# Attention logits: the low part of the keys against the high queries alone, on half the rows, two heads side by side

## The chip, the cores and the metric

The kernel runs on one NeuronCore of a Trainium2 chip. The metric is the device time of one execution in microseconds. TensorE (PE in the profile) does the matmuls, and its weight loads have a row of their own (PEld); VectorE (DVE), ScalarE (ACT) and GpSimd (POOL) work on rows of 128 partitions; SyncE (SP) issues most DMAs. Matmul results land in PSUM, which has eight banks of 512 fp32 columns.

## The reference

One layer on 1024 tokens of width 1024, in fp32: an input projection, an mLSTM mixer and a sparse attention mixer beside each other, a gated merge, and a feed-forward block. What matters here are the logits of the attention mixer. It has 8 heads of 64 dimensions in 2 groups that share keys; a block of queries is multiplied with three sets of keys (compressed, selected, windowed):

```python
q = q_in.reshape(B, T, G, R, dh).transpose(0, 2, 3, 1, 4) * (dh ** -0.5)
...
lc = (jnp.einsum('bgrqd,bgcd->bgrqc', qb, kc_).astype(jnp.float32)
      + table[:, :, rel_bucket(t[:, None] - cmp_end[None, :])])
...
ls = jnp.einsum('bgrqd,bgqnd->bgrqn', qb, k_g).astype(jnp.float32) + bias_s
...
lw = jnp.einsum('bgrqd,bgkd->bgrqk', qb, k_wb).astype(jnp.float32) + table[:, :, rel_bucket(dist)]
```

Each set goes through a masked softmax and is multiplied with its values; three gates weigh the sums. With 16 blocks of 64 keys and the 16 best chosen, all causal blocks are selected, so the selected branch is plain causal attention.

## The kernel before

**Precision.** Matmuls run in a rounded fp32 format (F32R), in which one pass is too coarse. So each operand is held as a high part (rounded) and a low part (the remainder), and a product is made of several passes: the dense products of three (lines 277 to 279), the logits of two. For the logits the queries' parts are stacked: in a tile QA of one head, rows 0 to 63 hold the high part of the 64 dimensions and rows 64 to 127 the low part (load_pair, line 1001). The keys are stacked twice: KH has the high part of the keys in both halves, KL the low part in both. A pass over 128 rows with KH gives (high q + low q) x high k, and a pass with KL gives (high q + low q) x low k.

**Units.** The attention stage (lines 1130 to 1499) works through 32 units: four pairs of heads, and in each the eight query blocks of 128 in the order 0, 7, 1, 6, 2, 5, 3, 4. A unit makes logits for two branches ("w": up to five blocks of windowed keys, with 64 compressed columns behind the last; "s": all blocks up to its own) and two heads (r = 0, 1). s_job (line 1145) allocates a score buffer of 1024 columns, which is two PSUM banks; there are two such buffers, used in turn. It issues the matmuls on lines 1164 and 1165, at most 512 columns each, so a block row of up to 640 or 1024 columns takes two pairs of them. Then VectorE adds the bias and finds the row's minimum (line 1191, low), ScalarE takes the exponential (line 1195), the rows are scaled, TensorE transposes them (line 1246), ScalarE and VectorE split the result in high and low (lines 1251 and 1255), and TensorE multiplies both with the values (lines 1266 and 1268).

**Order of the work.** A planner writes the order of each engine out before anything is issued. Every step is an Op with an engine, a cost in ns and dependencies; build_s and build_t (lines 1310 and 1356) make them, and a list scheduler (line 1455) takes the step that can start first, with a priority among those that can. When TensorE has nothing that can start within 120 ns, a piece of a dense product is placed instead: three matmuls of 512 columns of one of ten merge tiles (line 1430, c_dense, lines 277 to 279 with the tile name d). Six more merge tiles are computed after the stage. A score buffer comes free when low has read it: s_free keeps those steps, and the logits of the next head but one depend on them.

**Queues.** The QA and key tiles of the next pair are loaded through GpSimd's queue, and the bias tiles through SyncE's, when the last low of a pair is placed.

Of the kernel before, what the change touches and what calls it, by code (L numbers as in the profile page):

```python
# [8 lines left out]
F32 = mybir.dt.float32  # L9
# [5 lines left out]
P = 128  # L15
T = 1024
# [16 lines left out]
KB = 192  # L33
# [124 lines left out]
def body(ctx, tc, a, out, stop=None, dbg=None):  # L158
    nc = tc.nc
# [41 lines left out]
    d_q = [tc.dram_tile([P, 2, T], F32, name=f"d_q{j}") for j in range(4)]  # L201
# [104 lines left out]
    for nm, j in order_b1:  # L306
        c = {"kc": (C_KC, C_VC), "ks": (C_KS, C_KW)}[nm][j] if nm in ("kc", "ks") else colof[nm] + P * j
# [28 lines left out]
    with ExitStack() as sa:  # L336
# [12 lines left out]
        rows = ap_.tile([N_ROW, P], F32, name="rows")  # L349
# [638 lines left out]
    KS, QA, FB, FW = {}, {}, {}, {}  # L988
# [6 lines left out]
    def load_pair(p):  # L995
        g = p // 2
        for r in range(2):
            h = 2 * p + r
            q = kq.tile([P, T], F32R, name=f"QA{h}", tag=f"QA{r}", bufs=2)
            for z in range(2):  # L1000
                nc.gpsimd.dma_start(q[64 * z:64 * z + 64, :], d_q[p][64 * r:64 * r + 64, z, :])
            QA[h] = q
        if p % 2 == 0:
            for j in (1, 0):
                m = KB if j == 1 else P
                kh = kq.tile([P, NT, m], F32R, name=f"KH{g}{j}", tag=f"KH{j}", bufs=1)
                kl = kq.tile([P, NT, m], F32R, name=f"KL{g}{j}", tag=f"KL{j}", bufs=1)
                gs = slice(64 * g, 64 * g + 64)
                for t_, d_ in ((kh, d_kh), (kl, d_kl)):
                    for z in range(2):  # L1010
                        nc.gpsimd.dma_start(t_[64 * z:64 * z + 64, :, 0:P], d_[j][gs, :].rearrange("p (b c) -> p b c", c=P))
                KS[g, j] = (kh, kl)
            if g > 0:
                behind(g)
        for r in range(2):
            h = 2 * p + r
            f = kq.tile([P, T], F32, name=f"FB{h}", tag=f"FB{r}", bufs=1)
            w = kq.tile([P, 640], F32, name=f"FW{h}", tag=f"FW{r}", bufs=1)
            for t_, o_, n_ in ((f, 127, T), (w, FX + 127, 640)):
                d_ = d_rep[h][0:1, :]  # L1020
                nc.sync.dma_start(t_, bass.AP(tensor=d_.tensor, offset=d_.offset + o_, ap=[[RW - 1, P], [1, n_]]))
            FB[h], FW[h] = f, w
# [107 lines left out]
    with ExitStack() as sc:  # L1130
        cp = sc.enter_context(tc.tile_pool(name="stC", bufs=1, reuse_waits="tile"))
        psC = sc.enter_context(tc.tile_pool(name="psC", bufs=1, space=PSUM, reuse_waits="tile"))
# [6 lines left out]
        units = [(p, i) for p in range(4) for i in order]  # L1139
        NU = len(units)  # L1140
        nwin = lambda i: min(i + 1, 5)
        ncmp = lambda i: 8 * i + 7
        SUM, NXT, RS, EX = {}, {}, {}, {}

        def s_job(u, kind, r):

            p, i = units[u]
            g = p // 2
            cs = slice(P * i, P * i + P)
            if kind == "w" and r == 0:  # L1150
                NXT[u] = cp.tile([P, 2, 3], F32, name=f"nx{u}", tag="nx", bufs=3)
                SUM[u] = cp.tile([P, 2, 3], F32, name=f"sm{u}", tag="sm", bufs=3)
                RS[u] = cp.tile([P, 2, 3], F32, name=f"rs{u}", tag="rs", bufs=3)
            nx, sm = NXT[u], SUM[u]
            s = psC.tile([P, T], F32, name=f"S{u}{kind}{r}", tag="S", bufs=2)
            b = 1 if kind == "s" else 2
            kh, kl = KS[g, b - 1]
            q_ = QA[2 * p + r]
            e = cp.tile([P, T if b == 1 else 640], F32, name=f"E{u}{kind}{r}", tag="E" + kind, bufs=4)
            EX[u, kind, r] = e  # L1160
            f = FB[2 * p + r]

            def logits(o, k_, last):
                nc.tensor.matmul(o, q_[:, cs], k_(kh), start=True, stop=False)
                nc.tensor.matmul(o, q_[:, cs], k_(kl), start=False, stop=True)

            if b == 1:
                n, o0 = P * (i + 1), 0
                for c0 in range(0, i + 1, 4):
                    m = min(4, i + 1 - c0)  # L1170
                    logits(s[:, P * c0:P * (c0 + m)], lambda k: k[:, c0:c0 + m, :], False)
                rows_ = []
            else:

                nw = nwin(i)
                n, o0 = P * nw, P if nw == 4 else 0
                if nw > 1:
                    logits(s[:, o0:o0 + n - P], lambda k: k[:, i + 1 - nw:i, 0:P], False)
                logits(s[:, o0 + n - P:o0 + n - P + KB], lambda k: k[:, i, :], True)
                if r == 0:  # L1180
                    EX[u, "c"] = cp.tile([P, 2, P], F32, name=f"E{u}c", tag="Ec", bufs=3)
                ec, nn = EX[u, "c"], ncmp(i)
                nc.gpsimd.memset(ec[:, r, nn:P], 0.0)
                y0 = 31 + 16 * (56 - 8 * i)
                rows_ = [(ec[:, r, 0:nn], s[:, o0 + n:o0 + n + nn], f[:, y0:y0 + 16 * (nn - 1) + 1:16], r, 0)]
            bias = f[:, 896 - P * i:896 - P * i + n] if b == 1 or i < 4 else FW[2 * p + r]
            rows_.insert(0, (e[:, 0:n], s[:, o0:o0 + n], bias, r, b))

            def low():
                for e_, s_, f_, q, b in rows_:  # L1190
                    nc.vector.tensor_tensor_reduce(e_, s_, f_, 1.0, 1.0e29, ALU.add, ALU.min, nx[:, q, b:b + 1])

            def exp():
                for e_, s_, f_, q, b in rows_:
                    nc.scalar.activation(e_, e_, AF.Exp, bias=nx[:, q, b:b + 1], scale=-1.0, accum_out=sm[:, q, b:b + 1])

            return low, exp
# [96 lines left out]
        chain = {"S": [], "T": [], "V": []}  # L1294
# [3 lines left out]
        def push(op):  # L1298
            queues[op.eng].append(op)
            if op.alt:  # L1300
                queues[op.alt[0]].append(op)
            return op
# [4 lines left out]
        s_free = []  # L1307
        pair_at = {}

        def build_s(u):  # L1310
            p, i = units[u]
            ops = {}
            for k, r in (("w", 0), ("w", 1), ("s", 0), ("s", 1)):
                b = {"w": 2, "s": 1}[k]
                box = {}

                def emit(u=u, k=k, r=r, box=box):
                    box["low"], box["exp"] = s_job(u, k, r)


                if b == 1:
                    n, parts = P * (i + 1), [min(512, P * (i + 1) - c) for c in range(0, P * (i + 1), 512)]
                else:
                    n, parts = P * nwin(i), [P * (nwin(i) - 1)] * (nwin(i) > 1) + [KB]
                cost = 2 * sum(max(109.0, m / 2.4 + 13.0) for m in parts)
                deps = []
                if len(s_free) >= 2:
                    deps.append(s_free[-2])
                if u >= 2:
                    deps.append(("T", u - 2, b))  # L1330
                if u % 8 == 0 and k == "w" and r == 0:
                    deps.append(("pair", p))
                deps += chain["S"]
                so = push(Op("PE", cost, deps, emit, (u, 1)))
                chain["S"] = [so]
                nr, n = (2, n + ncmp(i)) if b == 2 else (1, n)
                tt = push(Op("DVE", nr * 180.0 + 1.044 * n, [so], lambda box=box: box["low"](), (u, 1)))
                s_free.append(tt)
                ex = push(Op("ACT", nr * 290.0 + 0.833 * n, [tt], lambda box=box: box["exp"](), (u, 1)))
                ops[k, r] = ex  # L1340
                if r == 1:
                    part = 0 if k == "w" else 1
                    de = [ops[k, 0], ex]
                    todo = scale(u, part)
                    rs = push(Op("DVE", 400.0, de, todo[0][0], (u, 2)))
                    bl = [2, 2, 0, 0] if part == 0 else [1, 1]
                    scd = {}
                    for bb, (fn, _) in zip(bl, todo[1:]):
                        nn = (ncmp(i), P * (i + 1), P * nwin(i))[bb]
                        scd.setdefault(bb, []).append(push(Op("DVE", 70.0 + 0.522 * nn, [rs], fn, (u, 2),  # L1350
                                                               alt=("ACT", 230.0 + 0.833 * nn))))
                    for bb, v in scd.items():
                        ops["sc", bb] = v
            return ops
# [100 lines left out]
        while any(queues.values()):  # L1455
            best = None
            for e in queues:
                cand = None
                for op in queues[e][:LOOK[e]]:
                    r = ready(op, e)  # L1460
# [645 lines left out]
    n = 0  # L2106
# [110 lines left out]
```

## Time and profile before

| what | value |
|---|---|
| time, median of 3 runs (lowest to highest) | 1573.76 us (1572.89 to 1574.58) |
| profiled execution, from its first to its last instruction | 1570.8 us |
| TensorE busy, matmuls | 7922 |
| attention stage, first logits to the last part of the tenth merge tile | 362.8 to 678 us |
| high-key passes (line 1164) and low-key passes (line 1165) | 216 each |
| transposes (line 1246) and value products (lines 1266, 1268) in that stage | 592, and 296 each |

A profile is one execution, and its span leaves out what lies before the first instruction and after the last; the runs' times hold that too. In the views, a matmul is shown from its start to a modelled end, which lies beyond the start of the next one, so the time that one takes from TensorE is read from start to start. PEld rows are the loads of the stationary operand, one for each matmul. A shape such as 128*63 beside a matmul gives the rows and columns of the stationary operand. In the order-in-time view the columns are the start in us, the length in us, the engine, the line, the operation, the tiles (written <- read), the shape and the count, and in brackets the idle time before it with what ended it. In the view by stretch, the columns are the stretch, its length, the busy time of each engine with the number of its instructions, the granted clock, and what the DMA engines moved.

### The profile page before, as it was taken

Reading aid. Unit: us, or ns where it says so; the run is one execution under the profiler, and the core shown is the slowest. Engines: PE = TensorE matmul, PEld = TensorE weight load, DVE = VectorE, ACT = ScalarE, POOL = GpSimd, SP = SyncE. Lnnn points to the kernel's source line nnn. Section 1 sums busy time; section 2 is a strip of 40 time slices with the busy share of each in tenths; the row PEclk is TensorE's granted clock in tenths of the full one; section 3 lists DMA queues with packets and bytes.
Section 4 is the critical chain, followed back from the end, with each engine's and each line's share of the span. In section 5 each row is a group of like instructions: output and inputs, shape, how many; then the busy total and the mean of one; then the engine's idle time right before and its main releaser. Section 6 shows DMA issues by size and latency. Waiting matters only on the chain.

```text
span 1570.8 us, 22156 instructions
## 1 busy us (share of the span) xinstructions
PE 1556.6 (99%) x7922; PEld 1318.7 (84%) x7922; DVE 1053.6 (67%) x2244; ACT 755.2 (48%) x1589; POOL 210.7 (13%) x345
## 2 busy tenths in 40 slices
PE   9999999999999999999999999999999999999997
PEld 7888888888998898888888888888888888888886
DVE  7446662237988787831566677666666666988996
ACT  5115555326888788842445363333333333454443
POOL 4013433430113010123001000000000000000130
PEclk9999999999999999999999999999999999999999
DMA  8107622592328232163556223222222223750302
GB/s 238 44 1 195 168 81 74 171 289 85 83 73 131 79 102 64 48 220 115 162 165 215 96 94 121 94 81 82 92 82 81 81 83 118 268 196 19 108 1 107
DMA packets 145868, 180.91 MB, mean 115 GB/s; under 512 B 9118, under 2 KB 103612, under 8 KB 145758
## 3 DMA queue, kind: packets, MB, share of 16 engines
q1 hardware_dynamic: 135900, 157.01, 32.5%
q0 software_dynamic: 9568, 22.16, 5.6%
q8 instruction: 62, 1.02, 0.3%
q14 instruction: 48, 0.39, 0.1%
q10 hardware_dynamic: 290, 0.33, 0.1%
HBM read 137.43 MB, written 49.90 MB: 119 GB/s over the span
## 4 chain that ended last, share of the span: by engine, by line
PE 95%; DVE 2%; DMA 1%; ACT 1%; issue 0%; POOL 0%; SPq 0%; DVEq 0%; ACTq 0%
PE PS L278 14%; PE PS L277 14%; PE PS L279 14%; PE d L277 9%; PE d L279 8%; PE d L278 8%; PE T L1246 4%; PE obank L1266 2%; PE obank L1268 2%; PE br L279 2%; PE br L277 2%; PE br L278 2%; PE PSA L277 1%; PE PSA L278 1%; PE PSA L279 1%; DVE acc L1649 1%
## 5 line engine op out<-in xcount | busy, mean ns | idle before, releaser
L277 PE MATMUL d<-UTH,whi 128*128 128x512 f32 x544 | 220.5, 405 | 1.0 <-ACT mg L1125 0.7
L279 PE MATMUL d<-UTH,wlo 128*128 128x512 f32 x544 | 212.9, 391 | 0.0
L278 PE MATMUL d<-UTL,whi 128*128 128x512 f32 x544 | 212.3, 390 | 0.0
L1649 DVE TENSOR_TENSOR sl<-PS,sl 128x512 f32<-128x512 f32 x182 | 123.6, 689 | 100.5 <-PE PS L279 100.1
L254 POOL TENSOR_TENSOR wlo<-raw,whi 128x256 fp32r<-128x256 f32 x120 | 93.1, 806 | 309.1 <-ACT whi L248 278.7
L1255 DVE TENSOR_TENSOR TL<-T,TH 128x512 fp32r<-128x512 f32 (+1 forms) x184 | 103.3, 582 | 31.8 <-ACT TH L1251 30.7
L279 PEld LDWEIGHTS d<-UTH,wlo 128*128 128x128 f32 x544 | 102.1, 188 | 22.5
L277 PEld LDWEIGHTS d<-UTH,whi 128*128 128x128 f32 x544 | 102.4, 188 | 17.8 <-ACT mg L1125 2.3
L278 PEld LDWEIGHTS d<-UTL,whi 128*128 128x128 f32 x544 | 102.6, 189 | 15.6
L1251 ACT ACTIVATE TH<-T 128x512 fp32r<-128x512 f32 (+1 forms) x184 | 90.2, 511 | 28.4 <-PE T L1246 25.7
L1649 DVE TENSOR_TENSOR sl<-sl,sl 128x512 f32<-128x512 f32 (+1 forms) x130 | 88.5, 688 | 22.0 <-DMA d_h<-sl 8.8
L1649 POOL TENSOR_TENSOR acc<-acc 128x512 f32<-128x512 f32 x6 | 9.2, 1550 | 618.5 <-DVE acc L1649 618.4
L1652 ACT ACTIVATE sl<-sl 128x512 f32<-128x512 f32 (+1 forms) x77 | 48.7, 633 | 57.5 <-PE PS L278 32.8
L1266 PE MATMUL obank<-TH,VHL 128*128 128x256 f32 x264 | 75.4, 309 | 0.0
L1268 PE MATMUL obank<-TL,VHL 128*128 128x256 f32 x264 | 68.2, 282 | 0.0
L277 PE MATMUL PS<-q 128*128 128x512 f32 x172 | 66.9, 389 | 0.0
L278 PE MATMUL PS<-q 128*128 128x512 f32 x172 | 66.9, 389 | 0.0
L279 PE MATMUL PS<-q 128*128 128x512 f32 x172 | 66.9, 389 | 0.0
L1652 ACT ACTIVATE q<-sl 128x512 fp32r<-128x512 f32 x74 | 43.1, 624 | 42.3 <-PE PS L278 32.1
L1607 DVE TENSOR_TENSOR q<-br,q 128x512 f32<-128x512 f32 x32 | 21.9, 688 | 55.6 <-ACT q L1595 36.7
L1652 ACT ACTIVATE wh<-sl 128x512 fp32r<-128x512 f32 x39 | 24.7, 633 | 58.4 <-PE PS L278 39.5
L1268 PEld LDWEIGHTS obank<-TL,VHL 128*128 128x128 f32 x264 | 50.2, 190 | 1.2 <-DVE TL L1255 0.3
(1314 smaller groups left out, 4330.9 us busy)
## 6 DMA issues: line engine op xcount, KB each, us to landing
raw<-in_w_in SPq DMA_DIRECT2D x33, 512.0 KB, 5.3
d_gu<-sl SPq DMA_DIRECT2D x44, 256.0 KB, 2.2
q<-d_mg SPq DMA_DIRECT2D x32, 256.0 KB, 3.2
d_rep<-d_row POOLq DMA_DIRECT2D x8, 960.0 KB, 11.7
sl<-in_w_down SPq DMA_DIRECT2D x15, 512.0 KB, 3.6
sl<-d_gu SPq DMA_DIRECT2D x15, 512.0 KB, 4.4
ra<-in_w_gate SPq DMA_DIRECT2D x14, 512.0 KB, 3.5
ra<-in_w_up SPq DMA_DIRECT2D x13, 512.0 KB, 3.6
```

Of the source, the lines that this page charges most:

```text
L254: nc.gpsimd.tensor_tensor(lo[:, zs], v[:, zs], cast32(hi)[:, zs], ALU.subtract)
L277: nc.tensor.matmul(ps, ah, bh, start=first, stop=False)
L278: nc.tensor.matmul(ps, ah, bl, start=False, stop=False)
L279: nc.tensor.matmul(ps, al, bh, start=False, stop=last)
L1246: nc.tensor.transpose(pt[:, z, P * r:P * r + P], e, ident)
L1251: nc.scalar.activation(hl[0][:, 0:m], pt[:, 0:m], AF.Copy)
L1255: nc.vector.tensor_tensor(hl[1][:, 0:m], pt[:, 0:m], cast32(hl[0])[:, 0:m], ALU.subtract)
L1266: nc.tensor.matmul(po, vv, th[:, z, :], start=(st[1] == 0), stop=False)
L1268: nc.tensor.matmul(po, vv, tl[:, z, :], start=False, stop=(st[1] == st[2]))
L1607: nc.vector.tensor_tensor(sg[b], ps, sg[b], ALU.mult)
L1649: return pl.step(alts, lambda e: ENG[e].tensor_tensor(out_(), x(), y(), alu), reads, writes, **kw)
L1652: return pl.step((("ACT", cost),), lambda e: nc.scalar.activation(out_(), x(), fn), reads, writes, **kw)
```

## The change

The pass of the low keys takes the high queries alone, over 64 rows instead of 128. The term low q x low k is no longer computed. For head r = 1 of a pair the halves of QA are exchanged when it is loaded: its high part now lies in rows 64 to 127, that of head 0 in rows 0 to 63 as before. So the low-key passes of the two heads use different halves of the array's rows, and they write different score buffers.

The logits of a unit and branch are issued in two steps of the planner. s_first opens the buffer of head 0 and makes its full pass with KH over 128 rows. s_rest opens the buffer of head 1, issues for each segment of columns the 64-row passes of head 0 and head 1 one after the other, and then the full pass of head 1. The planner gives the first step one pass's cost and the second two passes' plus 150 ns. s_first waits for the low of head 0 of the branch before, s_rest for that of head 1. Both low steps depend on s_rest. The windowed logits now lie in the score buffer so that the last block with the compressed keys always begins at column 512.

```diff
             for z in range(2):
-                nc.gpsimd.dma_start(q[64 * z:64 * z + 64, :], d_q[p][64 * r:64 * r + 64, z, :])
+                nc.gpsimd.dma_start(q[64 * (z ^ r):64 * (z ^ r) + 64, :], d_q[p][64 * r:64 * r + 64, z, :])
...
+        def segments(i, kind):
+            if kind == "s":
+                return 0, [(P * c0, min(4, i + 1 - c0), c0) for c0 in range(0, i + 1, 4)]
+            nw = nwin(i)
+            return 4 * P - P * (nw - 1), [(4 * P - P * (nw - 1), nw - 1, i + 1 - nw)] * (nw > 1) + [(4 * P, 0, i)]
+        def s_open(u, kind, r):
             p, i = units[u]
-            g = p // 2
-            cs = slice(P * i, P * i + P)
             if kind == "w" and r == 0:
                 NXT[u] = cp.tile([P, 2, 3], F32, name=f"nx{u}", tag="nx", bufs=3)
                 SUM[u] = cp.tile([P, 2, 3], F32, name=f"sm{u}", tag="sm", bufs=3)
                 RS[u] = cp.tile([P, 2, 3], F32, name=f"rs{u}", tag="rs", bufs=3)
+                EX[u, "c"] = cp.tile([P, 2, P], F32, name=f"E{u}c", tag="Ec", bufs=3)
+            EX[u, kind, r] = cp.tile([P, T if kind == "s" else 640], F32, name=f"E{u}{kind}{r}", tag="E" + kind, bufs=4)
+            SS[u, kind, r] = psC.tile([P, T], F32, name=f"S{u}{kind}{r}", tag="S", bufs=2)
+        def s_part(u, kind, r, rows, seg, start, stop):
+            p, i = units[u]
+            k_ = KS[p // 2, 1 if kind == "w" else 0][rows is not None]
+            rs = slice(0, P) if rows is None else slice(64 * rows, 64 * rows + 64)
+            o, m, b0 = seg
+            src, n = (k_[rs, b0:b0 + m, 0:P], P * m) if m else (k_[rs, b0, :], KB)
+            nc.tensor.matmul(SS[u, kind, r][:, o:o + n], QA[2 * p + r][rs, P * i:P * i + P], src, start=start, stop=stop)
+        def s_first(u, kind):
+            s_open(u, kind, 0)
+            for seg in segments(units[u][1], kind)[1]:
+                s_part(u, kind, 0, None, seg, True, False)
+        def s_rest(u, kind):
+            s_open(u, kind, 1)
+            segs = segments(units[u][1], kind)[1]
+            for seg in segs:
+                s_part(u, kind, 0, 0, seg, False, True)
+                s_part(u, kind, 1, 1, seg, True, False)
+            for seg in segs:
+                s_part(u, kind, 1, None, seg, False, True)
+        def s_job(u, kind, r):
+            p, i = units[u]
             nx, sm = NXT[u], SUM[u]
...
-            kh, kl = KS[g, b - 1]
-            q_ = QA[2 * p + r]
-            def logits(o, k_, last):
-                nc.tensor.matmul(o, q_[:, cs], k_(kh), start=True, stop=False)
-                nc.tensor.matmul(o, q_[:, cs], k_(kl), start=False, stop=True)
...
-                if nw > 1:
-                    logits(s[:, o0:o0 + n - P], lambda k: k[:, i + 1 - nw:i, 0:P], False)
-                logits(s[:, o0 + n - P:o0 + n - P + KB], lambda k: k[:, i, :], True)
...
-                cost = 2 * sum(max(109.0, m / 2.4 + 13.0) for m in parts)
-                deps = []
-                if len(s_free) >= 2:
-                    deps.append(s_free[-2])
-                if u >= 2:
-                    deps.append(("T", u - 2, b))
-                if u % 8 == 0 and k == "w" and r == 0:
-                    deps.append(("pair", p))
-                deps += chain["S"]
-                so = push(Op("PE", cost, deps, emit, (u, 1)))
-                chain["S"] = [so]
+                one = sum(max(109.0, m / 2.4 + 13.0) for m in parts)
+                if r == 0:
+                    deps = [s_free[-2]] if len(s_free) >= 2 else []
+                    if u >= 2:
+                        deps.append(("T", u - 2, b))
+                    if u % 8 == 0 and k == "w":
+                        deps.append(("pair", p))
+                    first = push(Op("PE", one, deps + chain["S"], lambda u=u, k=k: s_first(u, k), (u, 1)))
+                    rest = push(Op("PE", 2 * one + 150.0, [first] + s_free[-1:], lambda u=u, k=k: s_rest(u, k), (u, 1)))
+                    chain["S"] = [rest]
+                def emit(u=u, k=k, r=r, box=box):
+                    box["low"], box["exp"] = s_job(u, k, r)
+                    box["low"]()
                 nr, n = (2, n + ncmp(i)) if b == 2 else (1, n)
-                tt = push(Op("DVE", nr * 180.0 + 1.044 * n, [so], lambda box=box: box["low"](), (u, 1)))
+                tt = push(Op("DVE", nr * 180.0 + 1.044 * n, [rest], emit, (u, 1)))
                 s_free.append(tt)
                 ex = push(Op("ACT", nr * 290.0 + 0.833 * n, [tt], lambda box=box: box["exp"](), (u, 1)))
                 ops[k, r] = ex
```

More of the change, by code (lines that the diff above doesn't have):

```diff
@@ L1142, in body @@
         ncmp = lambda i: 8 * i + 7
-        SUM, NXT, RS, EX = {}, {}, {}, {}
-        def s_job(u, kind, r):
+        SUM, NXT, RS, EX, SS = {}, {}, {}, {}, {}
+        def segments(i, kind):
[4 more added lines that the diff above has]
+        def s_open(u, kind, r):
             p, i = units[u]
-            g = p // 2
-            cs = slice(P * i, P * i + P)
             if kind == "w" and r == 0:
@@ L1154, in s_job @@
+        def s_job(u, kind, r):
+            p, i = units[u]
             nx, sm = NXT[u], SUM[u]
-            s = psC.tile([P, T], F32, name=f"S{u}{kind}{r}", tag="S", bufs=2)
+            s, e, f = SS[u, kind, r], EX[u, kind, r], FB[2 * p + r]
             b = 1 if kind == "s" else 2
-            kh, kl = KS[g, b - 1]
-            q_ = QA[2 * p + r]
-            e = cp.tile([P, T if b == 1 else 640], F32, name=f"E{u}{kind}{r}", tag="E" + kind, bufs=4)
-            EX[u, kind, r] = e
-            f = FB[2 * p + r]
@@ L1163, in logits @@
-            def logits(o, k_, last):
-                nc.tensor.matmul(o, q_[:, cs], k_(kh), start=True, stop=False)
-                nc.tensor.matmul(o, q_[:, cs], k_(kl), start=False, stop=True)
-            if b == 1:
[L1168 to L1172, printed above, removed]
-            else:
-                nw = nwin(i)
-                n, o0 = P * nw, P if nw == 4 else 0
-                if nw > 1:
-                    logits(s[:, o0:o0 + n - P], lambda k: k[:, i + 1 - nw:i, 0:P], False)
-                logits(s[:, o0 + n - P:o0 + n - P + KB], lambda k: k[:, i, :], True)
-                if r == 0:
-                    EX[u, "c"] = cp.tile([P, 2, P], F32, name=f"E{u}c", tag="Ec", bufs=3)
+            o0 = segments(i, kind)[0]
@@ L1182, in s_job @@
+            rows_ = []
+            if b == 1:
+                n = P * (i + 1)
+            else:
+                n = P * nwin(i)
                 ec, nn = EX[u, "c"], ncmp(i)
@@ L1315, in build_s @@
                 box = {}
-                def emit(u=u, k=k, r=r, box=box):
-                    box["low"], box["exp"] = s_job(u, k, r)
                 if b == 1:
```

## The prediction

> **What bounds the kernel now.** I read the page first (span, busy time, chain), then the busy time by stretch inside the attention stage, then the waits of TensorE there, and last the order in time of single matmuls, because the price of this change hangs on the spacing between neighbours.
>
> ```profile
> span 1570.8 us, 22156 instructions
> PE 1556.6 (99%) x7922; PEld 1318.7 (84%) x7922; DVE 1053.6 (67%) x2244; ACT 755.2 (48%) x1589; POOL 210.7 (13%) x345
> PE 95%; DVE 2%; DMA 1%; ACT 1%; issue 0%; POOL 0%; SPq 0%; DVEq 0%; ACTq 0%
> 400.00:440.00 40.00, 40.00 (x276) 36.45 (x274) 34.04 (x115) 33.92 (x92) 5.93 (x16) 1.00 0.41 109
> sum 315.20, PE 314.20 PEld 281.82 DVE 256.39 ACT 252.82 POOL 48.53; mean PE 39.28 PEld 35.23 DVE 32.05 ACT 31.60 POOL 6.07
> PE d L277 <- ACT mg L1125: 0.7, 2, 0.4
> PEld d L277 <- ACT mg L1125: 2.3, 6, 0.5
> ```
>
> The first three lines are the page: 95% of the chain that ended last is TensorE. The next two are the stretches of the attention stage, from 362.8 us (the first logits) to 678 us: TensorE is busy for 314.2 of 315.2 us, VectorE for 256.4, ScalarE for 252.8, and the granted clock is 1.00. The last two are the longest waits of matmuls and of weight loads in this stage: 0.7 and 2.3 us in all. A busy matmul can hide a short gap, since a 512-column one is shown 0.39 us long while the next starts 0.23 us later, but nothing here is a long wait. So time that TensorE gains or loses in the stage goes to the end almost one for one, as long as VectorE (81% busy) keeps up. A gain of 17 us would bring VectorE to 256 of 298 us, so even that could pass through.
>
> The profiled span is 1570.8 us; the median of the three runs is 1573.76, which is 3.0 us more. I add 3.0 to every span.
>
> **What is removed.** The passes of the low keys on line 1165.
>
> ```profile
> 362.80:678.00 315.20, 65.17 (x216) 40.79 (x216) 1.00 0.34 81
> 368.72 0.39 PE L1165 MATMUL S1s<-KL,QA 128*128 128x512 f32 x1
> 368.95 0.39 PE L1164 MATMUL S1s<-KH,QA 128*128 128x512 f32 x1
> 644.64 0.34 PE L1165 MATMUL S30w<-KL,QA 128*128 128x384 f32 x1
> 644.82 0.25 PE L1164 MATMUL S30w<-KH,QA 128*128 128x192 f32 x1
> 644.91 0.28 PE L1165 MATMUL S30w<-KL,QA 128*128 128x192 f32 x1
> 645.02 0.27 PE L1246 MATMUL T<-cst,E28s 128*128 128x128 f32 x1
> 375.94 0.28 PE L1165 MATMUL S2s<-KL,QA 128*128 128x256 f32 x1
> 376.06 0.40 PE L277 MATMUL d<-UTH,whi 128*128 128x512 f32 x1
> 364.09 0.28 PE L1165 MATMUL S0s<-KL,QA 128*128 128x128 f32 x1
> 364.20 0.45 PE L277 MATMUL d<-UTH,whi 128*128 128x512 f32 x1
> ```
>
> The first line is the stretch view of line 1165 alone: 216 matmuls. Their busy time (65 us) overlaps their neighbours, so I count from one start to the next: 0.23 us for 512 columns, 0.18 for 384, 0.11 for 192, 0.12 for 256, 0.11 for 128. From the loops (query blocks 0 to 7, the windowed branch with up to five blocks and 64 compressed columns, the selected branch with block number plus one), a head of one pair has 10 matmuls of 512 columns, 3 of 384, 3 of 256, 8 of 192 and 3 of 128: 27, and 8 heads make the 216. Their time is 8 x (10 x 0.23 + 3 x 0.18 + 3 x 0.12 + 8 x 0.11 + 3 x 0.11) = 35.3 us. All of it is TensorE's own time.
>
> **What is added: the two heads side by side.** The same 216 matmuls come back with 64 rows each, in 108 couples. If both halves of a couple stream together, a couple costs what one pass did: 17.6 us back on. So 17.6 us is the most that this change can gain. If they do not run together it is 35.3 us back on and nothing gained; the trace of before has no matmul of 64 rows, so these are the ends, and I take the first: the operands lie in separate partitions and the results in separate score buffers, so I see nothing that the two share.
>
> **What is added: changing the shape of the array.** Each of the 64 calls of s_rest (32 units, two branches) goes from 128-row matmuls to 64-row ones and back. The trace has such detours, with other small shapes.
>
> ```profile
> 354.36 0.39 PE L278 MATMUL d<-UTL,whi 128*128 128x512 f32 x1
> 354.58 0.39 PE L279 MATMUL d<-UTH,wlo 128*128 128x512 f32 x1
> 354.90 0.44 PE L1103 MATMUL po<-w,hs 128*63 128x64 f32 x4
> 355.27 0.50 PE L277 MATMUL d<-UTH,whi 128*128 128x512 f32 x1
> 355.61 0.39 PE L278 MATMUL d<-UTL,whi 128*128 128x512 f32 x1
> ...
> 354.36 0.19 PEld L279 LDWEIGHTS d<-UTH,wlo 128*128 128x128 f32 x1
> 354.90 0.30 PEld L1103 LDWEIGHTS po<-w,hs 128*63 128x63 f32 x4 [0.35 <-issue]
> 355.27 0.19 PEld L277 LDWEIGHTS d<-UTH,whi 128*128 128x128 f32 x1
> 355.38 0.19 PEld L278 LDWEIGHTS d<-UTL,whi 128*128 128x128 f32 x1
> ...
> 119.84 0.39 PE L279 MATMUL d<-UTH,wlo 128*128 128x512 f32 x1
> 120.16 0.25 PE L812 MATMUL pq<-cst,gall 32*128 32x32 f32 x1
> 120.24 0.22 PE L813 MATMUL pq<-cst,gall 32*128 32x32 f32 x1
> 120.39 0.50 PE L277 MATMUL d<-UTH,whi 128*128 128x512 f32 x1
> 120.73 0.40 PE L278 MATMUL d<-UTL,whi 128*128 128x512 f32 x1
> ...
> 6.40 0.29 PEld L568 LDWEIGHTS G<-MV,ones 1*128 1x128 f32 x2
> 6.51 0.18 PEld L568 LDWEIGHTS G<-MV,ones 1*128 1x128 f32 x1
> ```
>
> Read the weight loads. Between equal shapes a load starts as soon as the matmul before begins (354.36, with the matmul of 354.36), so it is hidden. At a change of shape it starts only after that matmul is through: 354.90 against a slot that fell due at 354.58 + 0.23 = 354.81, so 0.09 us of nothing and then a load in the open; the same on the way back (load at 355.27, the next load 0.11 us later, the next matmul 0.34 after instead of 0.23). "Issue" as the reason says that no other engine was waited for. A whole detour: from 119.84 to 120.73 is 0.89 us, less two ordinary slots of 0.23 is 0.43, and the two 32-column matmuls in it are at most 0.08. From 354.58 to 355.61 is 1.03, less 0.46 is 0.57, and its four matmuls take some 0.22 (0.44 from the first start to the last end, less the 0.22 for which so short a matmul is shown, as on L813). Both leave about 0.35, the second with shorter loads; by parts it is 2 x (0.09 + 0.11) = 0.40. I take 0.38: 64 x 0.38 = 24.3 us.
>
> The Trainium skill, page "TensorEngine Tiling (Array Packing)", section Tiling Modes, says that changing the tiling mode, not merely the tile, drains the engine. The detours above agree with it, with about 0.09 us of nothing on each side; the page gives no figure, and it names no load left in the open, which in these rows costs as much again.
>
> **The second weight load of a couple.** Each half needs its own load. The nearest row is the last of the fence: two loads of L568 are 0.11 us apart. They go to the same rows of the array, so this is the upper end: 64 x 0.11 = 7.0 us (a couple that follows another inside a call loads under the streaming one). The lower end is nothing. I take a third, 2.4 us, since in my case the halves are separate.
>
> The Trainium skill, page "TensorE: Matmul & The Clock Gate", section "Part 3: Packing small matmuls", says that loads overlap with running matmuls when the row groups differ and that such matmuls start about 4 ns apart. By that rule the second load would cost nothing and the sum below would be 6.6 us instead of 9.0 (1580.4 us). No row here shows it.
>
> **What moves.** First and rest together still make one full pass per head. The rest waits until the reduction of the other head of the branch before has read its score buffer; behind it, in order, stand transposes, value products and merge tiles, and VectorE's line 1191 waits for it with both heads. Before, head 0 could be reduced while head 1's logits ran. The cost is between nothing and, if VectorE idles for one couple and its switch in each call (17.6 / 64 + 0.38 = 0.66 us), 42 us; I take nothing, because VectorE has 315.2 - 256.4 = 58.8 us of idle time and TensorE gets later, not earlier. If this cover went, TensorE would stand at the next rest. The changed partition of the QA loads issues the same 16 transfers; nothing for GpSimd's queue, and the planner's own arithmetic costs no time on the chip.
>
> Sum: -35.3 + 17.6 + 24.3 + 2.4 = +9.0 us, between +6.6 and +13.6 with the second load at its ends. Span 1579.8, time 1582.8 us.
>
> **The rivals.** *The switch is cheap.* The diff books 150 ns per call for it. Then 64 x 0.15 = 9.6 us against 17.6 gained: 8.0 us faster, 1565.8 us. Against it: no detour in the trace cost under 0.35 us. For it: none of them has 64 rows by 128 columns. It decides below 17.6 / 64 = 0.28 us per call. The Trainium skill's tiling page, section Overview, gives up to twice the speed for two row tiles; with the switch and the loads at nothing that is the full 17.6, or 1556.2 us. I give this side 0.17.
>
> *The halves do not run together.* Then nothing is gained and the calls pay the switches: -35.3 + 35.3 + 24.3 = +24.3, 1598.1 us. For it: no matmul in this trace is seen beside another. Against: separate rows and separate buffers. 0.12.
>
> *The tie of both heads stalls VectorE*, on top of the forecast: if a fifth of the 42 us shows, 8 us more, some 1591 us. For it: in the stretch quoted VectorE is at 34.0 of 40 us. 0.07.
>
> *It cancels.* A call costs about 0.28 us all told: 1573.8. 0.09.
>
> **How the numbers follow.** The forecast, 1582.8, has 0.55, and 1580 to 1588 is its own range. Together with the two slower rivals that is 0.74 for slower, 0.09 for the same, 0.17 for faster; 0.2% is 3.1 us, about what a measurement can tell. The range goes from 1566, the cheap switch, to 1597, just short of no overlap; what lies outside, the page's full gain and most of the second rival, is under 0.2.
>
> **What would show it.** Right: in the changed trace the first 64-row weight load of a call starts about 0.09 us after the slot at which a matmul was due, marked "issue"; the 128-row load behind the couples does the same; the two halves of a 512-column couple start less than 0.15 us apart and the next matmul follows in under 0.45; busy time of TensorE in the stage stays near all of it and the stage grows by some 9 us, nothing else moves. Wrong: loads hidden across the change of shape (cheap switch), halves 0.23 us apart (no overlap), or long idle rows of VectorE that end with the 64-row matmuls (the tie).

## The result, and the profile after

The changed kernel takes 1591.59 us (median of 4 runs, 1590.56 to 1593.14) against 1573.33 for the kernel before on the same chip: ratio 1.0114, 95% interval 1.01 to 1.0129, or 18.3 us slower. The forecast was 1582.8: the right side and inside the range, but half the size.

The first lines of the page after:

```profile
span 1590.5 us, 22155 instructions
PE 1568.1 (99%) x7922; PEld 1304.6 (82%) x7922; DVE 1064.0 (67%) x2248; ACT 751.2 (47%) x1585; POOL 212.2 (13%) x345
```

The stretch view of the attention stage in two parts, columns as before:

```profile
364.00:664.00 300.00, 296.95 (x1885) 244.37 (x1884) 237.49 (x767) 223.62 (x599) 49.60 (x124) 1.00 0.33 83
664.00:700.00 36.00, 30.31 (x209) 24.71 (x208) 29.43 (x83) 27.57 (x72) 0.29 (x2) 1.00 0.10 23
```

The longest waits of matmuls (PE) and of weight loads (PEld) in this stage, with the total, the count and the longest in us:

```profile
PE T L1262 <- DVE TL L1271: 3.2, 5, 1.2
PE d L277 <- ACT mg L1125: 1.3, 3, 0.6
PE S31s L1170 <- DVE nx L1207: 1.2, 1, 1.2
PE S4s L1170 <- DVE rs L1223: 1.0, 1, 1.0
PEld T L1262 <- DVE TL L1271: 5.5, 8, 1.4
PEld d L277 <- ACT mg L1125: 1.8, 3, 0.7
PEld S31s L1170 <- issue: 1.6, 2, 1.4
PEld S4s L1170 <- PE T L1262: 1.2, 1, 1.2
```

TensorE, which hardly waited before, now waits for VectorE's split (line 1255 before, 1271 now), and in the last 36 us of the stage it is idle for 5.7. Where the stage's time went is seen from the last merge tile inside it and the last output of the attention. These are the evictions of the merge tiles (line 1125) and the output copies (line 1274 before, 1290 after), of before and then of after; the numbers behind the count are the shortest, the median and the longest in ns, and the first and last start:

```profile
L1125 ACT ACTIVATE mg<-d,COLS x20: 687/689/692, 368.6 to 680.2; 128x512 f32<-128x512 f32 x20
L1274 ACT ACTIVATE os<-obank x32: 363/386/388, 373.1 to 677.4; 128x256 f32<-128x256 f32 x32
```

```profile
L1125 ACT ACTIVATE mg<-d,COLS x20: 687/688/692, 370.6 to 667.3; 128x512 f32<-128x512 f32 x20
L1290 ACT ACTIVATE os<-obank x32: 365/384/387, 374.2 to 698.9; 128x256 f32<-128x256 f32 x32
```

Before, fill and attention ended together, at 680 and 677 us. Now the fill is through at 667 and the attention only at 699; for 31 us nothing fills TensorE's holes. (Some 1.7 us of these shifts came in before the stage; see the last section.)

And one call of s_rest, the selected logits of unit 1 with two segments of 512 columns per head, matmuls and then weight loads in order of time (the first two low-key passes, then all four, from two windows of the same view):

```profile
371.94 0.40 PE L279 MATMUL d<-UTH,wlo 128*128 128x512 f32 x1
372.27 0.50 PE L1170 MATMUL S1s<-KL,QA 64*128 64x512 f32 x2
372.27 0.73 PE L1170 MATMUL S1s<-KL,QA 64*128 64x512 f32 x4
372.94 0.73 PE L1170 MATMUL S1s<-KH,QA 128*128 128x512 f32 x2
373.50 0.28 PE L1282 MATMUL obank<-TH,VHC 128*128 128x256 f32 x1
...
372.27 0.19 PEld L1170 LDWEIGHTS S1s<-KL,QA 64*128 64x128 f32 x2 [0.37 <-issue]
372.94 0.30 PEld L1170 LDWEIGHTS S1s<-KH,QA 128*128 128x128 f32 x2 [0.37 <-issue]
```

Two 64-row matmuls stand together in 0.50 us, the length of a single one with its load in the open, and two loads in 0.19, the length of one: the heads do run side by side, and so do their loads. The first load comes 0.10 us after the slot that fell due at 371.94 + 0.23, marked "issue"; the load of the full pass at 372.94 stands in the open too. From 372.17 to the working start of the full pass, 373.50 - 2 x 0.23 = 373.04, the call took 0.87 us for what four passes of 0.23 did in 0.92. This is the best case. Measured the same way from slot to slot, all 64 calls took 41.4 us in place of 35.3: some 6 us of the loss. In the rest of the stage, the time from each matmul's start to the next exceeds the median of its width before by 13.9 us in all; in the kernel before that sum is 3.0. So some 11 of the other 12 us are lost between matmuls elsewhere in the stage.

### The profile page after: what moved, and what is told of

It reads as the page before. It is cut to its first block, busy times and chain, and to the rows that moved or that the text cites. A ratio compares the mean times of both kernels' runs of the same rounds, so it can differ in the third digit from the quotient of the medians.

```text
span 1590.5 us, 22155 instructions
## 1 busy us (share of the span) xinstructions
PE 1568.1 (99%) x7922; PEld 1304.6 (82%) x7922; DVE 1064.0 (67%) x2248; ACT 751.2 (47%) x1585; POOL 212.2 (13%) x345
## 4 chain that ended last, share of the span: by engine, by line
PE 94%; DVE 3%; ACT 1%; DMA 1%; issue 1%; SPq 0%; DVEq 0%; ACTq 0%
PE PS L278 14%; PE PS L277 14%; PE PS L279 14%; PE d L277 8%; PE d L279 8%; PE d L278 8%; PE T L1262 4%; PE obank L1282 2%; PE obank L1284 2%; PE br L277 2%; PE br L278 2%; PE br L279 2%; PE PSA L277 1%; PE PSA L279 1%; PE PSA L278 1%; DVE acc L1664 1%
```

## The experiments

Unless another kernel is named, each difference is taken against the kernel before as measured beside that run (1573.96 us for the full rows, the same half and the two with one more tile; 1572.27 for the lows tied, the true cost, the cut with full rows and 64 rows alone; 1573.14 for the lows not tied and the two changed kernels with the cut; 1572.32 for the fill later).

**Full rows: the order alone.** The changed kernel, its low-key passes over 128 rows again.

```diff
-            rs = slice(0, P) if rows is None else slice(64 * rows, 64 * rows + 64)
+            rs = slice(0, P)
```

> The changed kernel with its low-key passes over all 128 rows again (all four products, as before the change), in the changed order: no 64-row matmul is left, so neither halves side by side nor changes of shape, but the two steps, the tie of both heads and the planner's costs stay. Theory (in the trace the 64 calls cost 6.2 us more than the passes they replace, and the other 12 us come from the order: the fill of merge tiles ends at 667 us and the attention runs on alone until 698): 1583 to 1588 us. Rival (the changes of shape are dearer than the spacings show, and the order is free): 1573 to 1576 us.

Measured: 1588.61 us, ratio 1.0097 (1.0081 to 1.0113), 14.6 us slower with no 64-row matmul at all. Its profile has the same tail as the changed kernel, first by the stretch, then by the last evictions and output copies:

```profile
664.00:700.00 36.00, 30.27 (x194) 25.77 (x193) 26.76 (x76) 24.77 (x64) 2.97 (x6) 0.95 0.13 29
```

```profile
L1125 ACT ACTIVATE mg<-d,COLS x20: 687/690/691, 369.9 to 663.0; 128x512 f32<-128x512 f32 x20
L1290 ACT ACTIVATE os<-obank x32: 362/383/387, 373.5 to 695.9; 128x256 f32<-128x256 f32 x32
```

The granted clock of 0.95 in the first line is 1.00 in the changed kernel: up to 36 x 0.05 = 1.8 us of this run's loss can be clock and not order. With that said, the order of the work, not the arithmetic, is the larger part of the loss.

**Same half: the halves cannot overlap.** Both heads' high queries in rows 0 to 63.

```diff
-                nc.gpsimd.dma_start(q[64 * (z ^ r):64 * (z ^ r) + 64, :], ...
+                nc.gpsimd.dma_start(q[64 * z:64 * z + 64, :], ...
-            rs = slice(0, P) if rows is None else slice(64 * rows, 64 * rows + 64)
+            rs = slice(0, P) if rows is None else slice(0, 64)
```

> The changed kernel with both heads' high queries in rows 0 to 63, so that the two 64-row passes of a couple use the same half and cannot stand beside each other; all else as changed. Theory (halves do stream together, worth half of the removed 35.3 us): 12 to 18 us slower than the changed kernel, 1603 to 1610 us. Rival (they gain nothing by lying in separate halves): 1590 to 1593 us.

Measured: 1606.99 us, ratio 1.0217 (1.0199 to 1.0235). The same call of unit 1 in its profile:

```profile
372.35 0.39 PE L279 MATMUL d<-UTH,wlo 128*128 128x512 f32 x1
372.67 1.19 PE L1170 MATMUL S1s<-KL,QA 64*128 64x512 f32 x4
373.79 0.50 PE L1170 MATMUL S1s<-KH,QA 128*128 128x512 f32 x1
```

Four 64-row passes span 1.19 us instead of 0.73. Against the changed kernel this is 15.4 us (14.8 if each is taken against the kernel before measured beside it): what the side-by-side is worth, near the 17.6 that it could be at most. Against the full rows it is 18.4 us, for 64 changes of shape there and back.

**One more merge tile inside the stage**, in the changed kernel and in the one before.

```diff
-NMC = 10
+NMC = 11
```

> The changed kernel with 11 instead of 10 merge tiles inside the attention stage (5 instead of 6 behind it). Theory (the attention's last 30 us wait for VectorE and ScalarE with nothing to fill them, about 9 us of idle TensorE): 1582 to 1586 us. Rival (the attention is longer everywhere, and a further merge tile only lengthens it): 1590 to 1593 us.

> The kernel before with 11 merge tiles inside the attention stage. Theory (its fill lasts to the end of the attention, only 3 us idle in all): 1572 to 1575 us, no change. Rival (one more tile of fill helps whatever the order): 1565 to 1569 us.

Measured: the changed kernel 1587.06 us, 1.0088 (1.0072 to 1.0104), so 4.5 us better than with ten; the kernel before 1575.63, 1.0014 (1.0004 to 1.0023), 1.7 us worse and a little above what I expected. So the changed order has idle time that fill can use and the one before has none, but one tile gets back less than I had expected.

**Lows tied, and not tied.** The code of the full rows, rearranged so that the first step makes all of head 0's passes and the second all of head 1's, with true costs. In the first run both reductions are planned behind the second step, in the other each behind its own.

```diff
             s_open(u, kind, 0)
             for seg in segments(units[u][1], kind)[1]:
                 s_part(u, kind, 0, None, seg, True, False)
+                s_part(u, kind, 0, 0, seg, False, True)
...
+                s_part(u, kind, 1, None, seg, True, False)
+                s_part(u, kind, 1, 1, seg, False, True)
...
-                tt = push(Op("DVE", nr * 180.0 + 1.044 * n, [rest], emit, (u, 1)))
+                tt = push(Op("DVE", nr * 180.0 + 1.044 * n, [rest if r else first], emit, (u, 1)))
```

The last pair of lines is the difference between the two runs; the first has the line with [rest].

> The order of the kernel before (each head makes its own passes with the high and the low keys over 128 rows, head 1 behind head 0, no 64-row matmul) with one part of the tie: the reductions of both heads are planned behind the second step. The planner's costs are the true ones. Theory (the order's 14.7 us come mainly from head 0 being reduced late): 1582 to 1588 us. Rival (they come mainly from head 0's low-key pass waiting for head 1's buffer): 1573 to 1577 us.

> The run with the lows tied, with that one dependency undone: head 0's reduction is planned behind the first step, head 1's behind the second. Everything else of the changed code stays that is neither the tie nor the 64-row passes (exchanged halves of the queries, the place of the columns in the score buffer, the logits and their reduction emitted in separate steps). Theory (these cost nothing, the tie does): 1572 to 1575 us. Rival (part of the order's cost is theirs): 1577 to 1586 us.

Measured: tied 1585.16 us, 1.0083 (1.006 to 1.0106), 12.9 slower; not tied 1573.09, 1.0002 (0.9993 to 1.0012). One dependency in the planner, with the same matmuls and the same bytes, costs 12 to 13 us. All the rest of the changed code (the exchanged halves, the place of the columns, the separate steps) costs nothing that can be measured.

The 12 us are not all of the kind that the changed kernel loses. This is the stretch from 520 to 540 us, where unit 16 begins and the second group's keys are loaded, of the tied, the untied and the changed kernel, and then two waits of the tied one there:

```profile
520.00:540.00 20.00, 16.91 (x77) 13.33 (x76) 5.88 (x32) 6.79 (x23) 5.46 (x15) 0.91 1.01 169
520.00:540.00 20.00, 19.64 (x121) 16.95 (x120) 16.31 (x71) 16.61 (x51) 3.70 (x11) 1.00 0.22 61
520.00:540.00 20.00, 19.83 (x121) 17.08 (x121) 9.20 (x27) 10.62 (x27) 4.18 (x9) 1.00 0.75 199
```

```profile
ACT mg L1125 <- DMA d_mg<-mg: 7.7, 1, 7.7
PE S16s L1170 <- DMA KL<-d_kl: 1.6, 1, 1.6
```

In the tied kernel TensorE is idle for 3.1 of the 20 us, behind the load of the keys and a merge tile's eviction that waits for the writing out of the one before, and at a clock of 0.91 it loses up to 1.8 more. The changed kernel has no such hole. So up to 5 of the 12 us come from one place in this order, and the run does not measure head 0's late reduction for the changed kernel.

**The planner's cost of the second step**, in the kernel with full rows.

```diff
-                    rest = push(Op("PE", 2 * one + 150.0, [first] + s_free[-1:], ...
+                    rest = push(Op("PE", 3 * one, [first] + s_free[-1:], ...
```

> The kernel of the run with full rows (changed order, all passes over 128 rows) with three passes as the planner's cost of the second step in place of two and 150 ns, which is what it really takes. Theory (the tie itself costs the 14.7 us, not the wrong cost in the planner): 1586 to 1590 us. Rival (the planner laid its fill wrongly because the cost was too low): 1574 to 1580 us.

Measured: 1585.22 us, 1.0085 (1.0065 to 1.0105), 12.9 slower in place of 14.6, a little below the expected range. The wrong cost is worth some 2 us by the medians; the intervals of the two runs overlap.

**The second step cut in two**, with full rows: low-key passes of both heads, then head 1's full pass; head 0 is reduced behind the first of these.

```diff
+                    mid = push(Op("PE", 2 * one, [first] + s_free[-1:], lambda u=u, k=k: s_rest(u, k), (u, 1)))
+                    rest = push(Op("PE", one, [mid], lambda u=u, k=k: s_last(u, k), (u, 1)))
...
+                tt = push(Op("DVE", nr * 180.0 + 1.044 * n, [rest if r else mid], emit, (u, 1)))
```

> The kernel of the run with full rows with the second step cut in two, the low-key passes of both heads and then the full pass of head 1, so that head 0's reduction is planned behind the first of these alone. The low-key pass of head 0 still waits for head 1's score buffer. True costs in the planner. Theory (head 0 being reduced late is the main part): 1575 to 1580 us. Rival (the wait for head 1's buffer is the main part): 1584 to 1590 us.

Measured: 1579.53 us, 1.0047 (1.0032 to 1.0063), 7.3 slower. The whole to compare with has true costs too: 12.9. So 5.6 us of the order's cost go when head 0 is reduced earlier; 7.3 stay, in a kernel where head 0's low-key pass still waits for head 1's buffer. The tie of the reductions alone (12.9, with the hole shown above) and this remainder (7.3) do not add up to the whole (12.9).

**64 rows alone, in the order of before:** the price of a change of shape.

```diff
-                nc.tensor.matmul(o, q_[:, cs], k_(kl), start=False, stop=True)
+                nc.tensor.matmul(o, q_[0:64, cs], k_(kl[0:64]), start=False, stop=True)
```

> The kernel before, order and costs unchanged, with each low-key pass on rows 0 to 63 alone (high queries x low keys, as in the change) directly behind its high-key pass: 216 changes of shape there and back, with no second head beside. Theory (a trip costs about 0.40 us: 0.09 us of nothing and a weight load of 0.11 in the open, both ways): 216 x 0.40 = 86 us more, 1650 to 1670 us. First rival (only the 0.09 us on each side, loads hidden): 216 x 0.18 = 39 us, 1605 to 1620. Second rival (150 ns a trip, as the planner books): 32 us, 1600 to 1608.

Measured: 1648.49 us, 1.0488 (1.0465 to 1.0512), 76.2 us for 216 trips there and back: 0.35 us each, a little below the expected range. Both rivals are out. In order of time, high-key and low-key passes in turn:

```profile
366.85 0.50 PE L1164 MATMUL S1w<-KH,QA 128*128 128x512 f32 x1
367.28 0.50 PE L1165 MATMUL S1w<-KL,QA 64*128 64x512 f32 x1
367.72 0.36 PE L1164 MATMUL S1w<-KH,QA 128*128 128x192 f32 x1
368.00 0.35 PE L1165 MATMUL S1w<-KL,QA 64*128 64x192 f32 x1
368.28 0.50 PE L1164 MATMUL S1w<-KH,QA 128*128 128x512 f32 x1
```

A 512-column pass now lasts 0.43 to 0.44 us to the next start and a 192-column one 0.28, in place of 0.23 and 0.11: 0.20 to 0.21 us for each change beside the wide pass, 0.17 beside the narrow one.

**The changed kernel with its second step cut in two**, with ten merge tiles and with eleven. The edit is the one with full rows, with one + 400.0 and one as costs.

> The changed kernel (64-row passes side by side) with the second step cut in two as in the run with the split: the low-key passes of both heads, then the full pass of head 1, and head 0's reduction planned behind the first. Costs in the planner: one pass and 400 ns, then one pass. Theory (the order's cost and the cost of the changes of shape add: 7.3 us are left of the order, 6.2 us for the shapes): 1583 to 1588 us. Rival (with the shapes changed, the cut of the second step brings nothing): 1590 to 1593 us. Neither expects it below the kernel before.

> The same with 11 merge tiles inside the attention stage, so that the fill lasts to its end. Theory (what is left of the order's cost is idle TensorE behind the fill): 1579 to 1583 us, near the 6.2 us of the shapes alone. Rival (what is left is spread over the stage): 1583 to 1588 us.

Measured: 1592.4 us, 1.0126 (1.0109 to 1.0143), with ten, so the rival: the cut that was worth 6 to 7 us with full rows brought nothing here. With eleven 1585.36, 1.0081 (1.0066 to 1.0096), 7 us better, but in the rival's range again. With ten, the fill ends 14 us before the attention, nearer than in the changed kernel (31 us), and yet nothing is gained:

```profile
L1125 ACT ACTIVATE mg<-d,COLS x20: 687/688/690, 370.5 to 685.7; 128x512 f32<-128x512 f32 x20
L1291 ACT ACTIVATE os<-obank x32: 362/384/388, 373.7 to 699.5; 128x256 f32<-128x256 f32 x32
```

```profile
PE d L277 <- ACT mg L1125: 4.5, 5, 2.3
```

The last line is from the waits of matmuls: those of the fill for the eviction of its one bank, 0.7 us in the kernel before, are 4.5 here. The trace shows where most of them stand, by the stretch at unit 16 and a wait in it:

```profile
520.00:540.00 20.00, 16.91 (x82) 12.98 (x79) 4.88 (x25) 6.60 (x20) 3.95 (x11) 0.91 0.93 236
```

```profile
ACT mg L1125 <- DMA d_mg<-mg: 6.8, 1, 6.8
```

As in the tied kernel, TensorE is idle for 3.1 us and the clock is 0.91, against 0.2 us and 1.00 in the changed kernel. That is up to 4.7 us more lost where the second group's keys are loaded, which can hide much of what the cut gains elsewhere. No run takes this hole away by itself, so how much the cut is worth with 64 rows stays open.

**Fill later**, in the changed kernel.

```diff
-                if cand is None or cand[2] > dst + 120.0:
+                if cand is None or cand[2] > dst + 400.0:
```

> The changed kernel with one number of the planner altered: a piece of a merge tile is placed only where TensorE would otherwise wait over 400 ns, instead of 120, so that the ten tiles of fill are used up later. Theory (the order's cost is the fill used up early by the small holes of the tie, and then idle TensorE): the fill lasts to the end of the attention, and 1579 to 1585 us. Rival (the tie makes the attention itself longer, wherever the fill stands): 1589 to 1594 us.

Measured: 1590.78 us, 1.0115 (1.0098 to 1.0132), no better. The fill did move:

```profile
664.00:700.00 36.00, 33.18 (x193) 27.81 (x191) 14.57 (x33) 14.48 (x30) 5.70 (x8) 1.00 0.18 48
```

```profile
L1125 ACT ACTIVATE mg<-d,COLS x20: 687/688/692, 370.5 to 699.7; 128x512 f32<-128x512 f32 x20
L1290 ACT ACTIVATE os<-obank x32: 358/383/386, 373.9 to 683.8; 128x256 f32<-128x256 f32 x32
```

The attention ended 15 us earlier, and merge tiles stood behind it instead; TensorE's idle time went from the tail to the holes that were no longer filled. So my picture that the fill is merely used up too early falls: placing the same fill later moves the idle time that the order makes and does not remove it. One more tile of fill did remove some of it (4.5 us above).

## Why the prediction was right and wrong

Step by step, by its own terms:

- *TensorE's time goes to the end one for one.* Right where the order stays: in the run with 64 rows alone the spacings, 0.17 to 0.21 us a change, make 73 to 91 us for 432 changes, and 76 arrived.
- *The halves side by side, 17.6 us saved.* Right: 15.4 (or 14.8) by the run with the same half.
- *The changes of shape, 64 x 0.38 = 24.3 us.* Right: 0.35 us a trip by the run with 64 rows alone, 22.6 us for 64; from slot to slot in the changed kernel 41.4 - 17.6 = 23.8 us, 0.37 a trip. The run with the same half ends only 18.4 us behind the full rows. Counted from start to start in the two traces, its calls cost 23.4 us more than full passes, while TensorE's other loss in the stage is 11.6 us in place of 17.3: together 17.7. So the rest falls where TensorE loses time anyway.
- *The second load, a third of 7.0 us.* Wrong, but small: both loads of a couple stand within the length of one, so it costs nothing. Two heads in separate rows are not like two loads for the same rows; there the trace agrees with the Trainium skill, page "TensorE: Matmul & The Clock Gate", section "Part 3: Packing small matmuls", which lets them overlap and has such matmuls start about 4 ns apart: here 88 of the 108 couples start 3 or 4 ns apart.
- These terms together gave 6.6 us with the second load at nothing; from slot to slot the trace shows 6.1.
- *What moves: "I take nothing, because VectorE has ... 58.8 us of idle time and TensorE gets later, not earlier".* This is the step that failed. The run with full rows has this term alone: 14.6 us. I had bounded it at 42 us and gave a fifth of that 0.07. Idle time in total is no cover for a tie: what counts is what can stand in the hole. By the code, head 0's next logits cannot be finished while head 1's buffer is read, and then both reductions come at once, with all that stands behind them; in the trace, TensorE waits for line 1271 where it waited for nothing, and 8.2 of the 13.9 us that it loses outside the calls stand behind the end of the fill. That the dependency is the cause is shown by undoing it: 12 to 13 us between the tied and the untied run, of which up to 5 are the hole at unit 16. For the kernel with full rows, planning head 0's reduction earlier gives back 5.6 of 12.9 us; the 7.3 left bound the wait for the other buffer. How the loss in the changed kernel divides between the two is not settled.

The steps from the kernel before over the full rows and the same half to the changed kernel (+14.6 for the order, +18.4 for the shapes, -15.4 for the overlap) sum to the measured change by the way they are taken, so that sum is no test. What bears the account out is the count in the changed kernel's own trace: 6.1 us in the calls and 10.9 more than before elsewhere in the stage.

That 1591.59 us lies inside the range is luck as far as this step goes: the upper end, 1597, was set by the rival without overlap, and nothing in the sum stood for the 12 us.

Of the rivals, the cheap switch is out (0.35 us against the 0.15 that the planner books, and against the 0.28 from which it would have paid); that the halves do not run together is out; the tie was there, beside the forecast and not instead of it. Its figure, some 1591, is what was measured, but by two errors that nearly cancel: 8 us for the tie where 12 came, on a sum of 9.0 where 6 came. Its sign, long idle rows of VectorE that end with the 64-row matmuls, showed only once: VectorE's waits for logits add up to 21.9 us in the stage against 13.6 before, and apart from one of 5.9 us at unit 16 none is above 1.8. The tie shows as TensorE waiting and as fill used up early. "Nothing else moves" was wrong: the fill ended 13 us earlier, and the attention 22 us later.

No version here beats the kernel before. A call gains only where the half that it saves is more than its trip; from slot to slot, of the thirteen sizes of call only the largest (1024 columns, 4 calls of 64) clearly does, by some 0.06 us.

## What to carry to other kernels

Halving an array pass pays only if the change of shape, there and back, is cheaper than the half: look in the trace for any matmul of odd shape among full ones and read its detour from start to start before counting the saving. When a change makes one step out of two that alternated on two buffers, cost the new dependency as a term of its own, by undoing it alone, and look in the trace for where its cost stands before carrying the figure over; the idle time of the engine that it delays, taken in all, did not bound it here. In a kernel whose order is written out ahead, another order can cost almost what the arithmetic gains: here 12 to 15 us against 15 to 18.

## What the runs showed that I had not expected

In the profiled execution of the changed kernel TensorE lost some 1.6 us at its very start, on instructions that are the same in both kernels. The stretch from 8 to 14 us, before and after:

```profile
8.00:14.00 6.00, 4.64 (x34) 4.02 (x34) 3.70 (x5) 4.30 (x7) 0.74 (x1) 1.00 1.04 362
```

```profile
8.00:14.00 6.00, 5.86 (x28) 4.62 (x26) 1.50 (x2) 0.54 (x2) 0.00 (x0) 0.72 1.04 357
```

The granted clock was 0.72 there against 1.00. The changed kernel with the cut and eleven tiles has 1.00 in the same stretch, and the four runs of the changed kernel spread over 2.6 us, so I do not put a part of that size in a difference of two profiles down to the change.

The clock also fell inside the attention stage, in the profiles of the full rows, the tied kernel and the changed kernel with the cut (0.95, 0.91 and 0.91 in the stretches shown above), and not in that of the kernel before (1.00). TensorE has idle time in each of those stretches, but so it has in the changed kernel's last 36 us, at a clock of 1.00; what lowers the clock was not tried.
